# Seven weight slots per layer split by GpSimd, and nine matmuls of zeros ahead of the first real one

## The chip, the cores and the metric

The kernel runs on one core of a Trainium2 chip. The time is that of the device for one execution, in microseconds; before the change the median of three runs is 840.27 us (839.91 to 840.84).

The core has five engines with queues of their own: TensorE (PE in the rows; its weight loads are PEld), VectorE (DVE), ScalarE (ACT), GpSimd (POOL) and SyncE (SP), which here only issues DMAs. Each works through its instructions in order, and waits on semaphores for the others.

## What is computed

A trunk of two layers over 512 tokens of width 1024, all in float32. Cut to the part that matters here:

```python
for l in range(DEPTH):                                   # 2
    h = x @ w_in[l]
    c_q, c_kv, k_r, gate_a, q_d, k_d, v_d, gate_b, gates = _split_cols(h)
    q_a = (_rms_norm(c_q, g_q[l]) @ w_q_up[l]).reshape(b, s, MLA_HEADS, MLA_NOPE + MLA_ROPE)
    ...
    kv = (_rms_norm(c_kv, g_kv[l]) @ w_kv_up[l]).reshape(b, s, MLA_HEADS, MLA_NOPE + MLA_V)
    ...
    o_a = _dense_attention(...)                          # 8 heads, latent attention
    y_a = o_a * jax.nn.silu(gate_a) @ w_branch_a[l]
    ...
    o_b = _differential_attention(...)                   # 4 heads, two softmax maps each
    y_b = _rms_norm(o_b, g_diff[l], eps=1e-5) * (1.0 - lam_init) * jax.nn.silu(gate_b) @ w_branch_b[l]
    merged = g[..., :D_MODEL] * y_a + g[..., D_MODEL:] * y_b
    x = _layer_norm(DEEPNORM_ALPHA * x + merged @ w_out[l], ln_gamma[l], ln_beta[l])
```

## The kernel before

Every float32 factor is kept as an upper part, rounded to the format that TensorE multiplies (F32R), and a lower part, which is the factor less its upper part. A product is then three matmuls (`mm3`, L140): upper by upper, upper by lower, lower by upper. So each weight and each intermediate has to be split: ScalarE copies it to the upper part, and another engine subtracts.

**Weights.** All large weights are packed into slots of 128 x 1024, named in `SLOTS`: ga0 to ga3 are the gate of the latent attention, qd and kd the queries and keys of the differential attention, kvup and qup the up-projections, vd, gb, gt, br and o the rest. `slot` (L124) loads a slot into a raw buffer `wr` (two of these), copies it to `wh` on ScalarE (L127) and subtracts twice, 512 columns each, into `wl` on VectorE (L130); `wh` and `wl` have three buffers each. `proj` multiplies a slot by x: 8 chunks of three matmuls. A raw buffer is free for the next load when the copy and both subtractions are done.

**Beginning.** VectorE clears a tile, and TensorE multiplies it with itself seven times (L110 and L111), before there is any input. Then, chunk by chunk of x and of the latent weights, `load_x` and `load_wc` load and split, and `project` runs twelve matmuls of 128 x 416 a chunk: four tiles of 128 tokens, three matmuls each.

**Latent stage.** For each tile of tokens ScalarE sums the squares (L255, L256), VectorE adds the epsilon (L257, L258), GpSimd raises to the power -0.5 (L259), and ScalarE and VectorE scale (L261, L262). Transposes follow.

**Attention.** The steps of the string `STEPS` run in the order in which they are written: Q, K, s, t and v are queries, keys, scores, transposes and values of the latent attention's heads, q, k, w and b load and project for the differential one, S, T and V are its attention, and g, m, G and M are gates and merges. The steps a1, q0, k0, q1, k1, a2 and a3, which load the slots of the change, stand among the latent attention's. A score tile goes from TensorE to VectorE (maximum, L196), ScalarE (exponential, L198), TensorE (transpose, L205), ScalarE and VectorE (split, L207 and L208), and TensorE again (L371, L372).

**Layer boundary.** The output columns are multiplied, VectorE normalizes each tile of tokens, with a power on GpSimd (L633), stores it, and `feature_major` (L643) transposes it, split into x's parts (L652, L653). The last two tiles of layer 0 are transposed between the projections of layer 1's first tiles.

**The order on the engines.** The code gives dependencies and the order of the steps; a scheduler of the framework then decides the order in which instructions stand on each engine. So a change of one instruction's engine also moves its neighbours.

GpSimd has had, until now, only the powers (L259, L478, L633) and the DMAs of `bcast` (L163, L167), which write a row of sums to memory and read it back to all partitions.

Of the kernel before, what the change touches and what calls it, by code (L numbers as in the profile page):

```python
# [14 lines left out]
ALU = mybir.AluOpType  # L15
# [50 lines left out]
def hybrid_trunk(ctx: ExitStack, tc: tile.TileContext, x, xT, wlat, wts, prm, dlam, gb, tab, rtab, out):  # L66
    nc = tc.nc
# [9 lines left out]
    def nm(s):  # L77
        uid[0] += 1
        return f"{s}_{uid[0]}"
# [3 lines left out]
    def t2(tag, dt=F32, w=512):  # L83
        return sb.tile([P, w], dt, tag=tag, name=nm(tag), bufs=BUFS[tag])
# [6 lines left out]
    def pt_(tag):  # L91
        return ps.tile([P, 512], F32, tag=tag, name=nm("ps" + tag), bufs=PB[tag])

    def fr(ap):
        return ap.bitcast(F32)
# [11 lines left out]
    zero = t2("p", mybir.dt.bfloat16)  # L107
    nc.vector.memset(zero, 0.0)
    warm = pt_("sc")
    for i in range(7):  # L110
        nc.tensor.matmul(warm, lhsT=zero[:, 0:P], rhs=zero, start=True, stop=True)  # L111

    xH = cst.tile([P, KC, SEQ], F32R, name="xH")
# [5 lines left out]
    def load(src):  # L119
        raw = t2("wr", F32, 1024)  # L120
        nc.sync.dma_start(raw, src)
        return raw

    def slot(l, name):  # L124
        raw = load(wts[l, SLOTS.index(name)])
        hi, lo = t2("wh", F32R, 1024), t2("wl", F32R, 1024)
        nc.scalar.copy(hi, raw)  # L127
        for i in range(0, 1024, 512):
            c = slice(i, i + 512)
            nc.vector.tensor_tensor(lo[:, c], raw[:, c], fr(hi[:, c]), ALU.subtract)  # L130
        return hi, lo


# [11 lines left out]
    def proj(l, name, tag="acc"):  # L145

        hi, lo = slot(l, name)
        acc = pt_(tag)
        for k in range(KC):
            mm3(acc, hi[:, k * P:(k + 1) * P], lo[:, k * P:(k + 1) * P],  # L150
                xH[:, k, :], xL[:, k, :], k == 0, k == KC - 1)
        return acc
# [58 lines left out]
    def layer(l, last):  # L211
# [207 lines left out]
        def diff_v(c):  # L419

            ws = [slot(l, f"vd{c}{i}") for i in range(2)]
            out = []
            for hf in range(2):
                acc = pt_("acc")
                for i in range(2):
                    tk = slice((2 * hf + i) * P, (2 * hf + i + 1) * P)
                    for k in range(KC):
                        o = (k % 4) * 256
                        mm3(acc[:, i * 256:(i + 1) * 256], xH[:, k, tk], xL[:, k, tk],
                            ws[k // 4][0][:, o:o + 256], ws[k // 4][1][:, o:o + 256], k == 0, k == KC - 1)  # L430
                out.append(split(acc, "kv"))
            return out
# [58 lines left out]
        def branch(which, c, ys):  # L491
            if c % 2 == 0:
                br[which] = slot(l, f"br{'AB'[which]}{c // 2}")
            bhh, bll = br[which]
            acc = pt_("acc")
            for k in range(4):
                o = ((c % 2) * 4 + k) * P
                mm3(acc, bhh[:, o:o + P], bll[:, o:o + P], ys[k][0], ys[k][1], k == 0, k == 3)
            return acc
# [258 lines left out]
def _build(arrays):  # L758
    import concourse.bacc as _bacc
    nc = _bacc.Bacc("TRN2", target_bir_lowering=False, num_devices=1)  # L760
    args = [nc.dram_tensor(f"in_{n}_dram", arrays[n].shape, F32, kind="ExternalInput").ap() for n in _INS]
    args.append(nc.dram_tensor("out_0_dram", (SEQ, DM), F32, kind="ExternalOutput").ap())
    with tile.TileContext(nc) as tc:
        hybrid_trunk(tc, *args)
    return nc
# [9 lines left out]
```

## Time and profile before

| | |
|---|---|
| median of three runs | 840.27 us |
| the profiled execution, its own time | 840.24 us |
| its span, first to last instruction | 838.3 us |
| mean granted TensorE clock | 0.998 |
| VectorE, all 192 subtractions of `slot` | 127.3 us |
| ScalarE, all 96 copies of `slot` | 101.1 us |
| GpSimd, busy in all | 47.1 us |

A row of a group reads: line, engine, operation, output <- inputs, shapes, count | busy time, mean ns of one | idle time of the engine ahead of them, and who ended it. A row of a timeline begins with start and duration in us. A row of a stretch is its bounds, its length and the busy time (and number of instructions) of TensorE, its weight loads, VectorE, ScalarE and GpSimd, then the granted clock, the share of the DMA engines, and GB/s. L with a number is the line of the kernel before.

Busy time of TensorE is modelled to each matmul's end, and matmuls overlap: a 128 x 512 one takes 389 ns by its row, and the next starts some 230 ns behind it.

### The profile page before, as it was taken

Reading aid. Unit: us, or ns where it says so; the run is one execution under the profiler, and the core shown is the slowest. Engines: PE = TensorE matmul, PEld = TensorE weight load, DVE = VectorE, ACT = ScalarE, POOL = GpSimd, SP = SyncE. Lnnn points to the kernel's source line nnn. Section 1 sums busy time; section 2 is a strip of 40 time slices with the busy share of each in tenths; the row PEclk is TensorE's granted clock in tenths of the full one; section 3 lists DMA queues with packets and bytes.
Section 4 is the critical chain, followed back from the end, with each engine's and each line's share of the span. In section 5 each row is a group of like instructions: output and inputs, shape, how many; then the busy total and the mean of one; then the engine's idle time right before and its main releaser. Section 6 shows DMA issues by size and latency. Waiting matters only on the chain.

```text
span 838.3 us, 11089 instructions
## 1 busy us (share of the span) xinstructions
PE 828.4 (99%) x4095; PEld 693.1 (83%) x4095; DVE 590.0 (70%) x1070; ACT 430.0 (51%) x858; POOL 47.1 (6%) x70
## 2 busy tenths in 40 slices
PE   9999999999999999999999999999999999999996
PEld 7878888888898878888898787798888988788885
DVE  6789989667656664555867899887576566455657
ACT  5777777544624653333336787674454355433310
POOL 0100000000000011000110000000000001100001
PEclk9999999999999999999999999999999999999999
DMA  8411121222223263333532120122222323623222
GB/s 288 125 60 45 45 69 58 82 76 76 76 88 101 63 226 110 96 96 121 181 113 76 50 62 16 64 64 84 93 68 83 95 69 109 219 88 110 94 74 101
DMA packets 29622, 79.96 MB, mean 95 GB/s; under 512 B 4000, under 2 KB 8704, under 8 KB 29568
## 3 DMA queue, kind: packets, MB, share of 16 engines
q1 hardware_dynamic: 27648, 75.01, 28.4%
q0 software_dynamic: 1920, 4.25, 1.5%
q8 instruction: 32, 0.52, 0.2%
q14 instruction: 22, 0.18, 0.1%
HBM read 74.99 MB, written 4.24 MB: 95 GB/s over the span
## 4 chain that ended last, share of the span: by engine, by line
PE 96%; DMA 2%; DVE 1%; ACT 1%; issue 0%; DVEq 0%; SPq 0%; ACTq 0%; POOLq 0%
PE psacc L141 23%; PE psacc L142 23%; PE psacc L143 23%; PE pstr L205 5%; PE pssc L141 2%; PE pssc L142 2%; PE pssc L143 2%; PE pspv L371 2%; PE pspv L142 2%; PE pspv L372 2%; PE pspv L143 2%; PE pspv L141 2%; DMA tmp<-rows 1%; PE pssc L440 1%; PE pssc L444 1%; PE pssc L445 1%
## 5 line engine op out<-in xcount | busy, mean ns | idle before, releaser
L130 DVE TENSOR_TENSOR wl<-wr,wh 128x512 fp32r<-128x512 f32 x192 | 127.3, 686 | 101.0 <-ACT wh L127 94.4
L141 PE MATMUL psacc<-xH,wh 128*128 128x512 f32 x496 | 194.9, 393 | 0.0
L142 PE MATMUL psacc<-xL,wh 128*128 128x512 f32 x496 | 194.4, 392 | 0.0
L143 PE MATMUL psacc<-xH,wl 128*128 128x512 f32 x496 | 193.7, 390 | 0.0
L127 ACT CAST wh<-wr 128x1024 fp32r<-128x1024 f32 x96 | 101.1, 1053 | 144.3 <-PE psacc L142 106.9
L141 PEld LDWEIGHTS psacc<-xH,wh 128*128 128x128 f32 x496 | 93.2, 188 | 19.2
L143 PEld LDWEIGHTS psacc<-xH,wl 128*128 128x128 f32 x496 | 93.2, 188 | 19.0
L198 ACT ACTIVATE p<-pssc,sm 128x512 f32<-128x512 f32 x128 | 87.7, 688 | 41.1 <-DVE sm L196 40.6
L142 PEld LDWEIGHTS psacc<-xL,wh 128*128 128x128 f32 x496 | 93.2, 188 | 18.5
L196 DVE TENSOR_REDUCE sm<-pssc 128x1 f32<-128x512 f32 x128 | 85.0, 683 | 13.8 <-PE pssc L441 10.7
L208 DVE TENSOR_TENSOR pt<-pstr,pt 128x512 fp32r<-128x512 f32 x96 | 64.8, 684 | 3.1 <-ACT pt L207 2.5
L207 ACT CAST pt<-pstr 128x512 fp32r<-128x512 f32 x96 | 55.5, 585 | 18.0 <-PE pstr L205 15.0
L205 PE MATMUL pstr<-ident,p 128*128 128x128 f32 x384 | 57.6, 272 | 0.0
L205 PEld LDWEIGHTS pstr<-ident,p 128*128 128x128 f32 x384 | 47.1, 140 | 11.3 <-ACT p L198 1.1
L143 PE MATMUL psacc<-wh,xL 128*128 128x256 f32 x128 | 36.3, 284 | 0.0
L142 PE MATMUL psacc<-wl,xH 128*128 128x256 f32 x128 | 36.3, 284 | 0.0
L141 PE MATMUL psacc<-wh,xH 128*128 128x256 f32 x128 | 36.3, 284 | 0.0
L505 ACT ACTIVATE tmp<-psacc,bh 128x512 f32<-128x512 f32 x32 | 21.9, 684 | 11.7 <-DVE g L483 7.7
L371 PE MATMUL pspv<-pt,vs 128*128 128x512 f32 x64 | 27.1, 423 | 0.0
L163 POOL DMA_DIRECT2D rows<-tmp x16 | 9.1, 567 | 307.9 <-ACT tmp L161 307.9
L372 PE MATMUL pspv<-pt,vs 128*128 128x512 f32 x64 | 26.1, 407 | 0.0
L141 PE MATMUL pssc<-kv,qm 128*128 128x512 f32 x64 | 26.0, 421 | 0.0
(297 smaller groups left out, 1628.0 us busy)
## 6 DMA issues: line engine op xcount, KB each, us to landing
wr<-in_wts_dram SPq DMA_DIRECT2D x106, 512.0 KB, 3.5
p<-in_xT_dram SPq DMA_DIRECT2D x8, 256.0 KB, 5.3
qr<-in_wts_dram SPq DMA_DIRECT2D x16, 128.0 KB, 2.0
tmp<-rows POOLq DMA_DIRECT2D x16, 128.0 KB, 3.0
tmp<-rows POOLq DMA_DIRECT2D x8, 256.0 KB, 3.7
p<-in_gb_dram SPq DMA_DIRECT2D x8, 256.0 KB, 3.6
y<-in_x_dram SPq DMA_DIRECT2D x8, 256.0 KB, 5.8
x_scratch<-y SPq DMA_DIRECT2D x8, 256.0 KB, 2.1
```

The source lines that it names most:

```text
L127: nc.scalar.copy(hi, raw)
L130: nc.vector.tensor_tensor(lo[:, c], raw[:, c], fr(hi[:, c]), ALU.subtract)
L141: nc.tensor.matmul(o, lhsT=lh, rhs=rh, start=start, stop=False)
L142: nc.tensor.matmul(o, lhsT=lh, rhs=rl, start=False, stop=False)
L143: nc.tensor.matmul(o, lhsT=ll, rhs=rh, start=False, stop=stop)
L196: nc.vector.tensor_reduce(m, S, axis=AX.X, op=ALU.max, negate=True)
L198: nc.scalar.activation(p, S, AF.Exp, bias=m, scale=1.0, accum_out=sums)
L205: nc.tensor.transpose(b[:, t * P:(t + 1) * P], pts[t][:, c * P:(c + 1) * P], ident)
L207: nc.scalar.copy(h, b)
L208: nc.vector.tensor_tensor(lo, b, fr(h), ALU.subtract)
L371: nc.tensor.matmul(pv, lhsT=v, rhs=ph, start=kc == 0, stop=False)
L372: nc.tensor.matmul(pv, lhsT=v, rhs=pl, start=False, stop=kc == NT - 1)
```

## The change

```diff
-    for i in range(7):
+    for i in range(9):
         nc.tensor.matmul(warm, lhsT=zero[:, 0:P], rhs=zero, start=True, stop=True)
...
+    LATENT = ("ga1", "ga2", "ga3", "qd0", "qd1", "kd0", "kd1")
+
     def slot(l, name):
         raw = load(wts[l, SLOTS.index(name)])
+        eng = nc.gpsimd if name in LATENT else nc.vector
         hi, lo = t2("wh", F32R, 1024), t2("wl", F32R, 1024)
         nc.scalar.copy(hi, raw)
         for i in range(0, 1024, 512):
             c = slice(i, i + 512)
-            nc.vector.tensor_tensor(lo[:, c], raw[:, c], fr(hi[:, c]), ALU.subtract)
+            eng.tensor_tensor(lo[:, c], raw[:, c], fr(hi[:, c]), ALU.subtract)
```

The lower parts of seven slots in each layer, 14 subtractions of 128 x 512 a layer and 28 in all, are made by GpSimd, and TensorE begins with nine matmuls of zeros. The values stay the same. In the changed file all lines behind `load` stand four lower: L130 becomes L134, L259 becomes L263.

The scheduler moves other instructions with them. GpSimd's rows at the layer boundary before, where `sm` are the small tiles of statistics (L633 the normalization's powers of four tiles of tokens, L259 the latent stage's) and `rows` is the first broadcast of layer 1:

```order
L633 TENSOR_TENSOR sm_3902<-sm_3902,mhalf 128x1
L633 TENSOR_TENSOR sm_3940<-sm_3940,mhalf 128x1
L633 TENSOR_TENSOR sm_3978<-sm_3978,mhalf 128x1
L633 TENSOR_TENSOR sm_4030<-sm_4030,mhalf 128x1
L259 TENSOR_TENSOR sm_4147<-sm_4147,mhalf 128x2
L259 TENSOR_TENSOR sm_4195<-sm_4195,mhalf 128x2
L259 TENSOR_TENSOR sm_4229<-sm_4229,mhalf 128x2
L259 TENSOR_TENSOR sm_4263<-sm_4263,mhalf 128x2
L163 DMA rows_4685<-tmp_4683 8x128
```

The same place on GpSimd in the change, where wl_4356 is the lower part of ga1, wl_4622 of qd0, and the last three of kd0, qd1 and kd1:

```order
L637 TENSOR_TENSOR sm_3980<-sm_3980,mhalf 128x1
L134 TENSOR_TENSOR wl_4356<-wr_4353,wh_4355 128x512 x2
L637 TENSOR_TENSOR sm_4032<-sm_4032,mhalf 128x1
L134 TENSOR_TENSOR wl_4622<-wr_4619,wh_4621 128x512
L263 TENSOR_TENSOR sm_4149<-sm_4149,mhalf 128x2
L134 TENSOR_TENSOR wl_4622<-wr_4619,wh_4621 128x512
L263 TENSOR_TENSOR sm_4197<-sm_4197,mhalf 128x2
L263 TENSOR_TENSOR sm_4231<-sm_4231,mhalf 128x2
L263 TENSOR_TENSOR sm_4265<-sm_4265,mhalf 128x2
L134 TENSOR_TENSOR wl_4799<-wr_4796,wh_4798 128x512 x2
L134 TENSOR_TENSOR wl_5035<-wr_5032,wh_5034 128x512 x2
L134 TENSOR_TENSOR wl_5212<-wr_5209,wh_5211 128x512 x2
```

The last power of the normalization now stands behind ga1's two subtractions, and the first two powers of the latent stage stand behind one half each of qd0's.

ScalarE's rows at the same place before, where psacc_4053 and psacc_4054 are the latent projections of the first two tiles of tokens, pstr_4132 and pstr_4139 the transposes of x's third tile, pstr_4180 and pstr_4187 of its fourth and last:

```order
L255 ACTIVATE qm_4146,sm_4147<-psacc_4053 128x128
L652 CAST xH<-pstr_4132 128x4x128
L652 CAST xH<-pstr_4139 128x4x128
L256 ACTIVATE qm_4146,sm_4147<-psacc_4053 128x256
L261 ACTIVATE qm_4146<-psacc_4053,sm_4147 128x128
L127 CAST wh_4619<-wr_4617 128x1024
L652 CAST xH<-pstr_4180 128x4x128
L652 CAST xH<-pstr_4187 128x4x128
L255 ACTIVATE qm_4194,sm_4195<-psacc_4054 128x128
L256 ACTIVATE qm_4194,sm_4195<-psacc_4054 128x256
```

The same place on ScalarE in the change (all buffer numbers are two higher):

```order
L259 ACTIVATE qm_4148,sm_4149<-psacc_4055 128x128
L260 ACTIVATE qm_4148,sm_4149<-psacc_4055 128x256
L656 CAST xH<-pstr_4134 128x4x128
L656 CAST xH<-pstr_4141 128x4x128
L131 CAST wh_4621<-wr_4619 128x1024
L265 ACTIVATE qm_4148<-psacc_4055,sm_4149 128x128
L259 ACTIVATE qm_4196,sm_4197<-psacc_4056 128x128
L260 ACTIVATE qm_4196,sm_4197<-psacc_4056 128x256
L656 CAST xH<-pstr_4182 128x4x128
L656 CAST xH<-pstr_4189 128x4x128
```

The copy of qd0's upper part (L131) now stands ahead of the first scaling (L265), which waits for GpSimd, and the copies of x's last tile stand behind that scaling and behind the squares of the second tile.

## The prediction

> **What bounds the kernel now.** The page of the profile comes first: the span, the busy times and the chain that ended last.
>
> ```profile
> span 838.3 us, 11089 instructions
> PE 828.4 (99%) x4095; PEld 693.1 (83%) x4095; DVE 590.0 (70%) x1070; ACT 430.0 (51%) x858; POOL 47.1 (6%) x70
> PE 96%; DMA 2%; DVE 1%; ACT 1%; issue 0%; DVEq 0%; SPq 0%; ACTq 0%; POOLq 0%
> ```
>
> TensorE is busy for 828.4 of 838.3 us and makes up 96% of the chain. VectorE, which the change relieves, is at 70% and off the chain. So a microsecond taken from VectorE is worth nothing by itself; it counts only where TensorE waits for it, or for somebody who waits for it. The profiled execution took 840.24 us, 1.94 us more than its span, and stands 0.03 us under the median of the runs, 840.27. The sum below is made against 840.24.
>
> Busy time hides how fast TensorE runs, so the timeline of its first ten microseconds comes next (start, duration, instruction).
>
> ```profile
> 1.23 3.17 PE L111 MATMUL pssc<-p 128*128 128x512 bf16 x7 [1.23 <-DVE p L108]
> 5.14 0.71 PE L141 MATMUL psacc<-kv,xH 128*128 128x416 f32 x1 [0.75 <-ACT xH L137]
> 5.66 0.55 PE L142 MATMUL psacc<-kv,xH 128*128 128x416 f32 x1
> 6.00 0.55 PE L141 MATMUL psacc<-kv,xH 128*128 128x416 f32 x1
> ...
> 9.12 0.55 PE L143 MATMUL pspv<-kv,xL 128*128 128x416 f32 x1
> 9.47 0.41 PE L141 MATMUL psacc<-kv,xH 128*128 128x416 f32 x1
> 9.72 0.35 PE L142 MATMUL psacc<-kv,xH 128*128 128x416 f32 x1
> 9.91 0.35 PE L143 MATMUL psacc<-kv,xL 128*128 128x416 f32 x1
> ```
>
> Seven matmuls of zeros run from 1.23 to 4.40, then TensorE stands 0.75 us for the first chunk of x, then real work starts at 5.14. Up to 9.12 it starts a matmul every 0.35 us (5.66 to 6.00), from 9.72 on every 0.19 (9.72 to 9.91), the same shape. So the clock rises near 9.5, 4.33 us after unbroken work began at 5.14, and twelve real matmuls run slowly. (The granted clock reads 1.00 in this stretch already; the distances of the starts are what I go by.)
>
> The third view is the busy time by stretch for the two stages in which the moved subtractions mostly lie, and one later stage.
>
> ```profile
> 45.00:147.00 102.00, 102.00 (x530) 83.60 (x529) 94.14 (x167) 76.37 (x163) 6.53 (x12) 1.00 0.17 54
> 460.00:561.00 101.00, 101.00 (x526) 82.41 (x525) 92.54 (x165) 75.23 (x161) 6.40 (x12) 1.00 0.17 53
> 147.00:250.00 103.00, 103.00 (x536) 88.04 (x535) 67.59 (x125) 47.72 (x92) 2.21 (x3) 1.00 0.26 81
> ```
>
> The columns are the stretch, its length, then TensorE, weight loads, VectorE, ScalarE and GpSimd. VectorE is 92% busy in the latent attention of each layer, yet TensorE shows no idle time there.
>
> **Part 1, two more matmuls of zeros.** Seven take 3.17 us, so one every 0.43; nine end their starts at 1.23 + 9 x 0.43 = 5.1, where the first real one, which waits for ScalarE's copy of x, begins at 5.14 anyway. They cost 0.05 us at most and fill the pause of 0.75 us. If the clock needs unbroken work for 4.33 us, as it did after 5.14, it now rises at 1.23 + 4.33 = 5.56 and one or two real matmuls are slow instead of twelve. A slow one costs 0.35 - 0.19 = 0.16 us more. The bounds are nothing saved (the zeros or the pause play no part) and 12 x 0.16 = 1.9 us. One execution shows one delay only, and the three times of before differ by 0.93 us, as if the rise moved between runs; I take three slow ones left, nine saved: **-1.4 us**.
>
> The Trainium skill, "TensorE: Matmul & The Clock Gate", Part 1, says that the clock is released after one window of about 3.4 us of sustained work, and that the windows run freely, whenever the kernel starts. By that rule the rise would come anywhere from 3.4 to 6.8 us after unbroken work begins; the 4.33 us of the trace agrees, and the sum of this part would be about -1.3 us in the mean of runs, with a spread of more than a microsecond between them.
>
> Is the faster start fed? What the second and third chunk (twelve matmuls each) wait for last is in VectorE's timeline.
>
> ```profile
> 7.13 0.59 DVE L226 TENSOR_TENSOR kv<-y,kv 128x416 fp32r<-128x416 f32 x1 [0.35 <-ACT kv L225]
> 9.08 0.59 DVE L226 TENSOR_TENSOR kv<-y,kv 128x416 fp32r<-128x416 f32 x1
> 16.70 1.29 DVE L138 TENSOR_TENSOR xL<-p,xH 128x512 fp32r<-128x512 f32 x2
> ```
>
> They are there at 7.72 and 9.67; at full speed from about 6 the chunks begin near 7.8 and 10.1. The last two chunks of x are there at 17.99; the seventh begins at about 7.8 + 5 x 12 x 0.19 = 19.2. It is fed, and as TensorE sets the pace behind it, the gain stays.
>
> **Part 2, 28 subtractions move to GpSimd.** What VectorE loses, from the page's group and from the timeline around the last moved slot of layer 0, ga3:
>
> ```profile
> L130 DVE TENSOR_TENSOR wl<-wr,wh 128x512 fp32r<-128x512 f32 x192 | 127.3, 686 | 101.0 <-ACT wh L127 94.4
> 108.62 0.68 DVE L130 TENSOR_TENSOR wl<-wr,wh 128x512 fp32r<-128x512 f32 x1
> 109.22 0.69 DVE L187 TENSOR_TENSOR y<-op,y 128x512 fp32r<-128x512 f32 x1
> 111.73 0.64 DVE L130 TENSOR_TENSOR wl<-wr,wh 128x512 fp32r<-128x512 f32 x1
> 118.58 0.48 PE L141 MATMUL psacc<-xH,wh 128*128 128x512 f32 x1
> ```
>
> One takes 0.69 us and hands over after 0.60: 14 a layer free 8.4 us, of which seven, 4.2 us, lie in each stretch above (the others lie at 19 to 45 and 416 to 448). What that frees on TensorE is bounded by what it loses to late waits there. A matmul of this size that waits for nothing takes 389 ns, and the same groups with and without waits are:
>
> ```profile
> L371 PE MATMUL pspv<-pt,vs 128*128 128x512 f32 x64 | 27.1, 423 | 0.0
> L372 PE MATMUL pspv<-pt,vs 128*128 128x512 f32 x64 | 26.1, 407 | 0.0
> L141 PE MATMUL pssc<-kv,qm 128*128 128x512 f32 x64 | 26.0, 421 | 0.0
> L143 PE MATMUL psacc<-lat,wl 128*128 128x512 f32 x64 | 24.9, 389 | 0.0
> L440 PE MATMUL pssc<-qm,qm 128*128 128x512 f32 x32 | 13.5, 421 | 0.0
> L141 PE MATMUL pspv<-pt,kv 128*128 128x512 f32 x32 | 13.3, 417 | 0.0
> ACT p L198 <- DVE sm L196: 12.1, 16, 1.4
> ```
>
> The first three lose 64 x (34 + 18 + 32) ns = 5.4 us in both layers. ScalarE does wait for VectorE there (12.1 us in the first stretch, last row), so there is a way for the relief to reach TensorE. But the next two groups are the same kinds of matmul in the differential attention, most of it in stages like the third stretch, where VectorE is at 66%, and they lose as much (421) or nearly (417). So these losses hardly hang on VectorE's load. Between 0 and 5.4 us I take **-0.5 us**, near the end that the rows support.
>
> What GpSimd gains has no row in this profile: a 128x512 subtraction of two inputs. The nearest are VectorE's 0.69 us, and GpSimd's own:
>
> ```profile
> 1.02 0.29 POOL masks.py:199 TENSOR_SCALAR_AFFINE_SELECT ident<-ident 128x128 f32<-128x128 f32 x1
> 422.31 0.98 POOL L633 TENSOR_TENSOR sm<-sm,mhalf 128x1 f32<-128x1 f32 x1 [5.99 <-DVE sm L632]
> 426.88 1.18 POOL L259 TENSOR_TENSOR sm<-sm,mhalf 128x2 f32<-128x2 f32 x1 [3.59 <-DVE sm L258]
> ```
>
> From 0.29 us for 128 columns and one input come 1.16 for 512, twice that for two inputs, and with 0.98 as a fixed part 3.3 us. So one takes 0.69 to 3.3 us; I take 1.3, near the scaled row. The Trainium skill, "GPSIMD Engine Reference", 3.1, has 4.5 us for a 2048-wide addition; a quarter of it, an estimate from that page, is 1.1 us.
>
> A slot then takes 2.6 us instead of 1.3, and the cover is wide: ga3's halves end at 109.30 and 112.37 and are used from 118.58 on, and GpSimd, busy for 6.5 of 102 us, can start as soon as the upper part is cast. The narrow place is the layer boundary, where ga1's and half of qd0's subtraction now stand on GpSimd ahead of the RMS powers (order rows above):
>
> ```profile
> 417.35 1.05 ACT L127 CAST wh<-wr 128x1024 fp32r<-128x1024 f32 x1 [0.19 <-DVE y L639]
> 424.86 0.68 DVE L130 TENSOR_TENSOR wl<-wr,wh 128x512 fp32r<-128x512 f32 x1
> 428.10 0.37 ACT L261 ACTIVATE qm<-psacc,sm 128x128 f32<-128x128 f32 x1 [2.28 <-POOL sm L259]
> 429.43 1.05 ACT L127 CAST wh<-wr 128x1024 fp32r<-128x1024 f32 x1 [0.96 <-DMA wr<-in_wts_dram]
> 430.38 1.07 ACT L652 CAST xH<-pstr 128x512 fp32r<-128x512 f32 x2
> 434.21 0.35 PE L141 MATMUL pspv<-kv,xH 128*128 128x416 f32 x1
> ```
>
> Before, ga1's second half ends at 425.54, which frees its raw buffer; qd0's load follows and its cast runs at 429.43, 3.9 us after. Now, with p for one subtraction: ga1's cast ends at 418.40, GpSimd at 418.40 + 2p, the load has landed at 422.3 + 2p. On ScalarE the cast (1.05), then after GpSimd's half (p) and the power (1.18) the scaling (0.37), two squares (about 0.75) and the copy of x's last tile (1.07) follow, which TensorE needs at 434.21: 422.3 + 3p + 4.4 = 434.2 gives p = 2.5. At 1.3 there are over 2 us to spare, also behind the earlier casts; at 3.3 TensorE stands 3 x 0.8 = 2.4 us, once. At 1.3 this costs **0**. The loads of later slots are released earlier than before, which moves only SP's work.
>
> Sum: 840.24 - 1.4 - 0.5 = **838.3 us**.
>
> **The rivals.** A: the clock does not answer, because the zeros or the pause do not count; then only the relief is left, 840.24 - 0.5 = 839.8. Against it speaks that the rise follows the unbroken work by 4.33 us. B: the relief reaches TensorE well, with ScalarE's 12 us of waiting for VectorE as its way: two thirds of 5.4, 835.2. Against it speak 421 and 417. C, on the other side: while GpSimd subtracts, VectorE's operations with two inputs stand for the whole of it. VectorE then loses p and gains 0.60 seven times a stretch, and has 102 - 94.14 = 7.86 us of idle time: this decides from p = 0.60 + 7.86 / 7 = 1.7 us on. At 2.0 it falls behind by 1.9 us a stretch, 3.9 in both, and TensorE with it: 840.24 - 1.4 + 3.8 = 842.6. For it speaks the 92%; against it that much of VectorE's time there is work on one input, a quarter of it in the reductions alone:
>
> ```profile
> L196 DVE TENSOR_REDUCE sm<-pssc 128x1 f32<-128x512 f32 x36 | 24.2, 683 | 1.4 <-PE pssc L143 1.1 <-PE pssc L445 0.2
> ```
>
> The Trainium skill, "SBUF — State Buffer", "Who interferes with whom", states this as a rule: a VectorE instruction with two SBUF inputs and a GpSimd one that reads SBUF exclude each other for the whole instruction; no run here shows it yet. D: the new order of TensorE's rows and some of C's stops eat gain and relief, 840.0.
>
> **How the numbers follow.** Forecast 56%, A 17%, B 9%, C 8%, D 10%. A measurement tells 0.2%, 1.7 us, from no change: faster is below 838.6, slower above 841.9. The forecast's own range, 837.2 to 839.5, lies two thirds below 838.6, 37%; with B's 9 and 2 of A faster gets 48%. Slower is C, 8%; the rest, 44%, is the same. The range leaves out B and C, 17%: from 836.0, about halfway to B, to 841.2, which is the layer boundary's stop of 2.4 us at p = 3.3 with the relief lost (840.24 - 1.4 + 2.4).
>
> **What would show it.** Part 1: TensorE's starts 0.19 us apart from 5 to 7 us on, instead of 9.7, with no pause ahead of 5.14; the latent projection ends 1.4 us earlier. Part 2: 28 rows on POOL of 1.1 to 1.5 us each, L371 and L141 within a few ns of 423 and 421, and x's last tile copied ahead of its matmul at the layer boundary. Subtractions over 1.7 us, or VectorE's two-input rows longer than 0.69 us beside GpSimd's, would speak for C; slow starts still at 9 us for A.

## The result, and the profile after

| | before | the change |
|---|---|---|
| median, same chip | 840.13 us | 851.33 us (850.63 to 851.88, 4 runs) |
| ratio | | 1.0135, 95% interval 1.0123 to 1.0147 |
| profiled execution, own time | 840.24 us | 850.63 us |
| its span | 838.3 us | 848.8 us |

The change makes the kernel 11.2 us slower. Forecast were 838.3 us, 836.0 to 841.2. One execution of all those behind the tables of this document is left out, of 4389.4 us, in the run with qd0 of layer 0 and ga2 back.

The page of the change, span, busy times and chain:

```profile
span 848.8 us, 11108 instructions
PE 833.4 (98%) x4097; PEld 691.5 (81%) x4097; DVE 580.4 (68%) x1042; ACT 429.2 (51%) x858; POOL 84.0 (10%) x98
PE 87%; DVE 4%; DMA 2%; ACT 1%; issue 1%; DVEq 0%; SPq 0%; POOLq 0%; POOL 0%; ACTq 0%
L134 POOL TENSOR_TENSOR wl<-wr,wh 128x512 fp32r<-128x512 f32 x28 | 38.0, 1374 | 105.1 <-ACT wh L131 85.7
```

VectorE has 9.6 us less to do, and yet it now holds 4% of the chain instead of 1%: TensorE waits for an engine that is less busy than before. One subtraction on GpSimd takes 1.37 us in the mean, as guessed (1.3). The list of TensorE's waits in the change names the places (us in total, times, longest; the wait ahead of the zeros, 1.2 us as before, isn't shown):

```profile
PE pstr L296 <- DVE tmp L293: 2.4, 1, 2.4
PE pstr L209 <- DVE pt L212: 2.2, 2, 1.1
PE psacc L145 <- DVE tmp L349: 0.7, 1, 0.7
PE pspv L146 <- DVE pt L212: 0.6, 2, 0.5
```

Of these, the same list of before has only the fourth (0.8 us there). The longest stands at 29 us, in the beginning of layer 0. Its rows in the change's timeline (start, duration), and the two-input group of the same line before:

```profile
28.95 2.56 POOL L134 TENSOR_TENSOR wl<-wr,wh 128x512 fp32r<-128x512 f32 x2 [1.42 <-ACT wh L131]
29.16 2.51 DVE L293 TENSOR_TENSOR tmp<-tmp,tmp 128x128 f32<-128x128 f32 x2
31.72 0.63 PE L296 MATMUL pstr<-ident,tmp 128*64 128x128 f32 x4 [2.38 <-DVE tmp L293]
...
32.73 0.63 PE L147 MATMUL psacc<-xH,wl 128*128 128x512 f32 x1
33.15 0.63 PE L145 MATMUL psacc<-xH,wh 128*128 128x512 f32 x1
33.58 0.63 PE L146 MATMUL psacc<-xL,wh 128*128 128x512 f32 x1
```

```profile
30.80 0.48 DVE L289 TENSOR_TENSOR tmp<-tmp,tmp 128x128 f32<-128x128 f32 x2
```

Two additions of 128 columns, both inputs in SBUF, take 2.51 us beside the subtractions of qd0, and 0.48 without; the group ends at 31.67, 0.16 us behind GpSimd's pair (31.51). TensorE stands 2.38 us for them, and behind that its matmuls start 0.43 us apart (33.15 to 33.58) where 0.23 is usual: the clock has fallen to half.

The second place is ga2, in both layers alike. Rows of the change at 82 us, and of before where the same rotation (four lines lower in its numbers) stands:

```profile
81.67 2.98 POOL L134 TENSOR_TENSOR wl<-wr,wh 128x512 fp32r<-128x512 f32 x2 [8.31 <-ACT wh L131]
81.95 1.55 DVE L395 TENSOR_TENSOR tmp<-tmp,tabs 128x512 f32<-128x512 f32 x1
83.43 0.68 DVE L349 TENSOR_TENSOR tmp<-psacc,tabs 128x512 f32<-128x512 f32 x1
84.03 1.18 DVE L398 TENSOR_TENSOR tmp<-tmp,tmp 128x512 f32<-128x512 f32 x1
84.37 0.39 PE L146 MATMUL psacc<-lat,kv 128*128 128x512 f32 x1
85.86 0.66 PE L209 MATMUL pstr<-ident,p 128*128 128x128 f32 x4 [1.11 <-DVE pt L212]
```

```profile
77.90 0.68 DVE L391 TENSOR_TENSOR tmp<-tmp,tabs 128x512 f32<-128x512 f32 x1
79.10 0.68 DVE L394 TENSOR_TENSOR tmp<-tmp,tmp 128x512 f32<-128x512 f32 x1
```

The operation with two inputs in SBUF (L395) takes 1.55 instead of 0.68 us and so does not end before GpSimd's first subtraction has; L349, with one input in PSUM, runs at its usual 0.68 in the middle of GpSimd's second; L398, two inputs in SBUF again, waits for the second's end. GpSimd's pair is lengthened too, 2.98 instead of 2.56. The two lengthenings, 0.87 and 0.50 us, bring VectorE 1.4 us late to the next lower part (L212), and TensorE's starts lie 85.86 - 84.37 = 1.49 us apart instead of 0.23.

A third chain shows at 36 to 47 us, layer 0 alone, in the change's timeline over four engines:

```profile
36.20 2.55 POOL L134 TENSOR_TENSOR wl<-wr,wh 128x512 fp32r<-128x512 f32 x2 [4.68 <-ACT wh L131]
38.77 7.64 SPq L121 DMA_DIRECT2D wr<-in_wts_dram  x3
42.32 1.05 ACT L131 CAST wh<-wr 128x1024 fp32r<-128x1024 f32 x1 [1.37 <-DMA wr<-in_wts_dram]
43.28 0.57 ACT L324 CAST vs<-psacc 128x512 fp32r<-128x512 f32 x1
46.29 0.68 DVE L349 TENSOR_TENSOR tmp<-psacc,tabs 128x512 f32<-128x512 f32 x1
47.11 0.47 PE L145 MATMUL psacc<-lat,qw 128*128 128x512 f32 x1 [0.68 <-DVE tmp L349]
```

GpSimd ends kd0's pair at 38.75 and only then frees the raw buffer; SyncE issues the next load at 38.77, ScalarE waits 1.37 us for it in order to cast qd1, and the four copies of the values (L324), which the change's order puts behind that cast (in the second trace of before, three of the four stand ahead of it), wait with it, then VectorE's part of them, then TensorE. That this stop is GpSimd's doing alone isn't shown: in the runs below in which GpSimd only fills, and the raw buffer is free as soon as ScalarE has cast it, TensorE waits 0.6 to 0.7 us for the same product.

### The profile page after: what moved, and what is told of

It reads as the page before. It is cut to its first block, busy times and chain, and to the rows that moved or that the text cites. A ratio compares the mean times of both kernels' runs of the same rounds, so it can differ in the third digit from the quotient of the medians.

```text
span 848.8 us, 11108 instructions
## 1 busy us (share of the span) xinstructions
PE 833.4 (98%) x4097; PEld 691.5 (81%) x4097; DVE 580.4 (68%) x1042; ACT 429.2 (51%) x858; POOL 84.0 (10%) x98
## 4 chain that ended last, share of the span: by engine, by line
PE 87%; DVE 4%; DMA 2%; ACT 1%; issue 1%; DVEq 0%; SPq 0%; POOLq 0%; POOL 0%; ACTq 0%
PE psacc L147 22%; PE psacc L146 21%; PE psacc L145 21%; PE pstr L209 4%; PE pssc L145 2%; PE pspv L375 2%; PE pssc L146 2%; PE pssc L147 2%; PE pspv L376 2%; PE pspv L146 2%; PE pspv L147 1%; PE pspv L145 1%; DMA tmp<-rows 1%; PE pssc L448 1%; PE pssc L444 1%; PE pssc L445 1%
## 5 line engine op out<-in xcount | busy, mean ns | idle before, releaser
L131 ACT CAST wh<-wr 128x1024 fp32r<-128x1024 f32 x96 | 101.0, 1053 | 154.7 <-PE psacc L146 115.7
L134 DVE TENSOR_TENSOR wl<-wr,wh 128x512 fp32r<-128x512 f32 x164 | 108.3, 686 | 99.5 <-ACT wh L131 93.5
L212 DVE TENSOR_TENSOR pt<-pstr,pt 128x512 fp32r<-128x512 f32 x96 | 64.6, 683 | 4.5 <-ACT pt L211 3.8
L134 POOL TENSOR_TENSOR wl<-wr,wh 128x512 fp32r<-128x512 f32 x28 | 38.0, 1374 | 105.1 <-ACT wh L131 85.7
L482 POOL TENSOR_TENSOR sm<-sm,mhalf 128x4 f32<-128x4 f32 x8 | 9.8, 1228 | 228.5 <-DVE sm L480 228.4
L375 PE MATMUL pspv<-pt,vs 128*128 128x512 f32 x64 | 27.0, 422 | 0.5 <-ACT pt L211 0.2
```

The costliest lines, as they stand in the source:

```text
L134: eng.tensor_tensor(lo[:, c], raw[:, c], fr(hi[:, c]), ALU.subtract)
L212: nc.vector.tensor_tensor(lo, b, fr(h), ALU.subtract)
L375: nc.tensor.matmul(pv, lhsT=v, rhs=ph, start=kc == 0, stop=False)
```

## The experiments

Two theories stood against each other. The **hold**: while GpSimd reads SBUF in a subtraction, VectorE's operations with two inputs in SBUF stand until it ends (with the later release of raw buffers as its companion). The **order**: the scheduler, given other durations, places matmuls of TensorE ahead of what feeds them.

All runs, each beside the kernel before on the same chip:

| run | time | before | ratio, 95% interval |
|---|---|---|---|
| before, again | 838.97 | 838.68 | |
| nine zeros alone | 839.42 | 839.00 | 1.0005 (0.9996 to 1.0015) |
| GpSimd alone, seven zeros | 851.61 | 839.00 | 1.0146 (1.0131 to 1.0161) |
| qd0 of layer 0 back | 847.27 | 839.00 | 1.0096 (1.0081 to 1.0111) |
| qd0 of layer 0 and ga2 back | 844.01 | 839.42 | 1.0056 (1.0039 to 1.0073) |
| GpSimd copies one input | 844.67 | 839.00 | 1.0065 (1.0048 to 1.0081) |
| pieces of 128 columns | 853.33 | 838.68 | 1.0177 (1.0162 to 1.0192) |
| transposes in the pause | 851.41 | 839.42 | 1.0145 (1.0128 to 1.0162) |
| old order, GpSimd subtracts | 849.14 | 838.68 | 1.0122 (1.0107 to 1.0137) |
| old order, GpSimd fills | 846.10 | 839.42 | 1.0080 (1.0059 to 1.0102) |
| the same, GpSimd's order too | 840.91 | 839.57 | 1.0021 (1.0011 to 1.0030) |
| new order, GpSimd fills | 843.96 | 839.42 | 1.0056 (1.0041 to 1.0071) |
| new order, VectorE subtracts | 849.27 | 838.68 | 1.0123 (1.0106 to 1.0140) |

### The zeros alone, and before once more

```diff
-    for i in range(7):
+    for i in range(9):
```

> The kernel before with nine matmuls of zeros and nothing else. My reading of the changed kernel's first ten microseconds is that this part works: the clock rises at 5.25 instead of 9.59 us, and the starts of the first 10 us lose 1.84 instead of 4.28 us. So 840.2 - 2.4 = 837.8 us, between 837.4 and 838.9. If the early clock is worth nothing because later stages wait for something else, 840.2. If the loss of the change came from the zeros, near 851.

> The kernel before, unchanged, for a second trace. If the rise of the clock hangs on the pause ahead of the first real matmul, it comes near 9.6 us again and the first 10 us lose about 4.4 us. If it moves between executions, as the same seven zeros with a rise at 6.53 us in the run without the two further ones suggest, it may come anywhere from 4.7 to 9.6 us, and then the two zeros bring nothing that can be measured, as their run alone shows (839.42 against 839.0 us).

Nothing: the two zeros alone move the time by +0.4 us, not told from none. The second trace of before suggests why. Its timeline of TensorE:

```profile
1.22 3.17 PE L112 MATMUL pssc<-p 128*128 128x512 bf16 x7 [1.22 <-DVE p L109]
4.71 0.71 PE L142 MATMUL psacc<-kv,xH 128*128 128x416 f32 x1 [0.32 <-ACT xH L138]
5.57 0.54 PE L142 MATMUL psacc<-kv,xH 128*128 128x416 f32 x1
5.92 0.39 PE L143 MATMUL psacc<-kv,xH 128*128 128x416 f32 x1
6.52 0.35 PE L142 MATMUL psacc<-kv,xH 128*128 128x416 f32 x1
6.70 0.35 PE L143 MATMUL psacc<-kv,xH 128*128 128x416 f32 x1
...
30.19 0.52 PE L293 MATMUL pstr<-ident,tmp 128*64 128x128 f32 x3 [0.47 <-DVE tmp L290]
```

With the same seven zeros the starts are 0.35 us apart at 5.57 and 0.18 at 6.52: the clock rises near 6, and not at 9.5 as in the execution on which the prediction stood. The pause ahead of the first real matmul is 0.32 us here and was 0.75 there. And where TensorE comes early to 29 us, it waits 0.47 us for the rotated keys; with nine zeros, whose list of waits follows, 0.6:

```profile
PE pstr L292 <- DVE tmp L289: 0.6, 1, 0.6
```

### GpSimd alone

```diff
-    for i in range(9):
+    for i in range(7):
```

> The change without its two further zeros: only the subtractions on GpSimd. If the two parts add up, 851.3 + 2.4 = 853.7 us. If the stop of 2.4 us at 29 us depends on TensorE arriving there 2 us earlier than before, it shrinks to about 0.5 us, the clock does not fall behind it, and the time is 853.7 - 1.9 - 1.6 = 850.2 us or less. If GpSimd's subtractions cost nothing, 840.

851.61 us, +12.6: the loss is that of the moved subtractions. The clock rose early here as well, near 6.5 us, so TensorE didn't come to 29 us two microseconds later, and the second case of the expectation wasn't tried: it waits 2.3 us there. The busy time by stretch (the granted clock is the third number from the end):

```profile
25.00:36.00 11.00, 8.68 (x48) 7.10 (x47) 8.22 (x20) 7.35 (x20) 4.43 (x5) 1.00 0.22 69
45.00:52.00 7.00, 5.48 (x17) 4.08 (x17) 6.61 (x13) 3.63 (x9) 1.22 (x1) 0.76 0.36 115
```

After nearly the same pause as in the change (2.32 us instead of 2.38) the clock stays up here, and falls one stop later; the last section says where the two pauses differ.

### Slots taken back

```diff
-        eng = nc.gpsimd if name in LATENT else nc.vector
+        eng = nc.gpsimd if name in LATENT and (l, name) != (0, "qd0") else nc.vector
```

> The changed kernel with one slot, qd0 of layer 0, back on VectorE. By the theory that VectorE's operation with two inputs stands for the whole of GpSimd's pair, the stop of 2.4 us at 29 us and the half clock behind it (1.6 us) are gone, and perhaps the two later waits of 0.8 and 0.6 us that layer 1 doesn't have: 851.3 - 4.0 = 847.3 down to 845.9 us; the two-input group at 29 us takes 0.5 instead of 2.51 us. If the new order of the engines costs the time, one slot of 14 brings about 1 us at most: 850.3 to 851.3.

Two subtractions of 28 taken back bring the loss from 11.2 to 8.3 us, near the theory's 847.3; the clock stays up. The two-input group at 29 us takes 0.49 us, as expected; TensorE still waits 1.0 us for it, as VectorE's own subtraction of qd0 now stands ahead of it. With ga2 back as well:

```diff
+        eng = nc.gpsimd if name in LATENT and name != "ga2" and (l, name) != (0, "qd0") else nc.vector
```

> The changed kernel with qd0 of layer 0 and ga2 of both layers back on VectorE, the three pairs at 29, 82 and 499 us. If these holds make most of the loss, 847.3 (qd0 alone) less the two waits of 1.1 us and the blips behind them (1.3 each): 844.7 us. If other holds take their place, or the loss lies in the order, 846 to 848 us.

844.0 us, against 844.7 expected: 4.6 us are left, while 22 subtractions are still on GpSimd. So three pairs make more than half of the loss. What remains isn't in the holds at 29 and 82 us. (The scheduler places other instructions anew in both runs, so they don't part the hold from the order by themselves.)

### What holds VectorE

```diff
+            if name in LATENT:
+                nc.gpsimd.tensor_copy(lo[:, c], fr(hi[:, c]))
```

> The changed kernel with GpSimd copying the upper part where it subtracted, so with one input instead of two; the lower parts of these slots are wrong. If what holds VectorE is that both engines read two inputs, no operation of VectorE's is longer beside GpSimd, the stops at 29, 84 and 501 us go, and the time is 851.3 - 2.4 - 1.6 - 2.6 = 844.7 us or less. If any reading of GpSimd's holds VectorE, the rows at 29 and 82 us are as long as GpSimd's pair of copies, whatever that takes. If the order of the engines costs the time, 851 as before, with no long rows.

The time is that of the first case, but the rows are those of the second. Rows of GpSimd and VectorE in this run:

```profile
30.75 1.27 POOL L135 CAST wl<-wh 128x512 fp32r<-128x512 f32 x2 [1.40 <-ACT wh L131]
30.97 1.19 DVE L296 TENSOR_TENSOR tmp<-tmp,tmp 128x128 f32<-128x128 f32 x2
```

A copy with one input holds VectorE's two-input operations as well, 1.19 instead of 0.48 us; it just takes half as long as the subtraction. The idea that both engines must read two inputs falls: on GpSimd's side one is enough. With zeros filled in, where GpSimd only writes, the same group runs at its own pace beside it (the last of the runs below, in the old order with GpSimd's order too):

```profile
29.56 0.99 POOL L184 MEMSET wl<- 128x512 f32 x2 [0.25 <-PE pssc L199]
29.99 0.49 DVE L345 TENSOR_TENSOR tmp<-tmp,tmp 128x128 f32<-128x128 f32 x2
```

This is the rule of the Trainium skill, "SBUF — State Buffer", "Who interferes with whom", that the prediction named: a VectorE instruction with two SBUF inputs and a GpSimd instruction that reads SBUF, not one that only writes it, exclude each other. These rows agree in both halves.

Cutting the subtractions up:

```diff
+        n = 128 if name in LATENT else 512
+        for i in range(0, 1024, n):
```

> The changed kernel with GpSimd's subtractions cut into pieces of 128 columns, eight instead of two a slot. If an operation of VectorE with two inputs waits for the end of one GpSimd instruction, it now waits for a quarter of the time: the wait at 29 us falls from 2.4 to about 1 us, the clock stays up (1.6), the waits at 84 and 501 us fall from 1.2 to about 0.4 us: 851.3 - 1.4 - 1.6 - 1.6 = 846.7 us. If VectorE gets through only when GpSimd has no more work, the waits stay and the time is 851 us or, since more instructions take longer, above.

Rows of VectorE, TensorE and ScalarE in this run:

```profile
29.27 0.90 DVE L294 TENSOR_TENSOR tmp<-tmp,tmp 128x128 f32<-128x128 f32 x2
30.23 0.63 PE L297 MATMUL pstr<-ident,tmp 128*64 128x128 f32 x4
44.86 1.04 ACT L131 CAST wh<-wr 128x1024 fp32r<-128x1024 f32 x1 [4.69 <-DMA wr<-in_wts_dram]
```

The mechanism is as expected: the hold lasts for one instruction of GpSimd's, so the group takes 0.90 us and the stop at 29 us is gone. The time is not: eight pieces take 3.4 to 3.9 us where two take 2.56, the raw buffer comes free later, and ScalarE's cast of qd1 now waits 4.7 us for its load, with the copies of the values behind it. TensorE stands 4.0 us there and the clock falls with it (0.66 over 45 to 55 us). The third chain, 0.7 us of waiting in the change, is the dearest here.

### The half clock

```diff
+        for _ in range(20 if l == 0 else 0):
+            nc.tensor.transpose(b[:, 0:P], ident, ident)
```

> The changed kernel, in its own order, with 20 transposes of the identity ahead of the rotated keys' (L300), where TensorE stands 2.4 us for VectorE; they write where the real ones write afterwards. They take 2.2 us, so TensorE works where it stood, and goes on no sooner. If the half clock from 32.6 to 36.0 us follows from the pause, it is gone and the time falls by 1.6 us: 849.7 us on a chip where the change takes 851.3, and 0.5 to 1.6 less in the mean if not every execution loses the clock. If the clock falls for another reason, nothing changes, or it rises by a few tenths.

No gain. The busy time by stretch in the change:

```profile
25.00:36.00 11.00, 8.62 (x39) 6.84 (x38) 8.08 (x20) 7.13 (x19) 4.04 (x5) 0.84 0.24 73
45.00:52.00 7.00, 6.32 (x28) 4.57 (x26) 6.61 (x15) 3.46 (x9) 1.06 (x1) 1.00 0.38 115
```

and with the transposes:

```profile
25.00:36.00 11.00, 11.00 (x68) 9.59 (x67) 8.03 (x20) 7.15 (x18) 4.00 (x5) 1.00 0.20 73
45.00:52.00 7.00, 5.48 (x18) 4.07 (x17) 6.38 (x13) 2.86 (x6) 1.05 (x1) 0.76 0.36 115
```

In the change the clock is 0.84 over 11 us, 11 x 0.16 = 1.8 us lost. With TensorE busy in the pause it stays at 1.00. But that the transposes did this isn't shown: in the run of GpSimd alone the clock stayed at 1.00 as well, with the pause of 2.32 us left as it was. What both runs show is the next stop. At 45 to 47 us TensorE waits 1.52 us for the same product of VectorE's instead of 0.68, because that chain runs over GpSimd, SyncE and ScalarE and not over TensorE, and behind this wait the clock falls there (0.76 over 7 us, 1.7 us). Two stops in a row, each on a chain of its own: what is saved at the first is lost again at the second.

### Order and hold apart

The change gives 855 of TensorE's 4097 matmuls another place than the nine zeros alone do. To part this from the hold, edges between neighbours keep TensorE, ScalarE and VectorE in a given order, whichever engine subtracts; `ORDER` is a table of instruction names, of the nine zeros alone (old) or of the change (new).

```diff
+def keep_order(tc):
+    by = {i.name: i for i in tc.nc.cur_bb.bb.instructions}
...
+            if prev is not None:
+                tc.add_manual_dep(ins, prev.name, info, reason="order")
+            prev = ins
...
         hybrid_trunk(tc, *args)
+        keep_order(tc)
```

> The change with the order of the kernel before: edges hold TensorE, ScalarE and VectorE to the very order that they have when VectorE subtracts all slots and nine zeros stand ahead, while GpSimd makes the 28 subtractions. What is left is GpSimd's hold on VectorE. By the theory of the hold: the wait at 29 us is 2.4 instead of 0.6 us (+1.8), the half clock behind it +1.6 where it falls, the waits at 82 and 499 us +1.2 each, so 839.4 + 5.8 = 845.2 us (843 to 847). If the new order made the loss: 839.4 us. If both do: what this run lacks to 851 is the order's.

> The other half: all subtractions on VectorE and nine zeros, but TensorE, ScalarE and VectorE are held to the order that the change gave them (only the 28 subtractions find their own place on VectorE). No GpSimd subtraction, so no hold. By the theory of the hold the order costs little: 839.4 plus the small losses of 0.2 to 0.3 us that the change shows in both layers alike, 1.5 and 2.0 us in the run with copies: 840.5 to 843 us. If the order is the cause, it is near 850 us. Since VectorE has its subtractions back, it may come later than in the change's own order would have it, which would add to this.

Both lose as much as the change: +10.5 and +10.6 us. The first shows that the new order isn't needed for the loss. It also lies above the 843 to 847 expected: in the old order the holds strike at more places, kd1's among them in both layers, here on GpSimd and VectorE:

```profile
65.48 3.04 POOL L182 TENSOR_TENSOR wl<-wr,wh 128x512 fp32r<-128x512 f32 x2 [18.62 <-ACT wh L179]
67.29 1.78 DVE L443 TENSOR_TENSOR tmp<-tmp,tabs 128x512 f32<-128x512 f32 x1
```

The second, expected at 840.5 to 843, misses: an order made for a relieved VectorE suffers when VectorE has the work back (in the same order, with VectorE relieved and GpSimd only filling, 4.5 us are lost below and not 10.6), so that run doesn't give the order's share. For that, GpSimd fills with zeros and reads nothing, in either order:

```diff
+            if name in LATENT:
+                nc.gpsimd.memset(fr(lo[:, c]), 0.0)
```

> As the run with the order of the kernel before (849.1 us), but GpSimd fills the 28 half slots with zeros where it subtracted, so it reads nothing; the lower parts of these slots are left out. VectorE has no more work than there. If the loss comes from what GpSimd's reading does (VectorE's two-input operations stand, the raw buffers come free later), all of it goes: 839.4 us, or down to 838 if VectorE's relief is worth something. If it comes from GpSimd's being late or from the change in VectorE's load, it stays near 849.

> The same with the order that the change gave to TensorE, ScalarE and VectorE: VectorE is relieved, as that order assumes, and nothing holds it. If the order itself costs nothing, 839.4 us as in the run before this; if its small losses of 0.2 to 0.3 us are its own, 840.5 to 842; if the order makes the change's loss, about 850.

In the new order +4.5 us remain, between the second and the third case; GpSimd's own rows aren't held in that run, but TensorE waits nowhere in it for more than 0.7 us behind the beginning. The run in the old order, 846.1 us instead of 839.4, had two stops for which GpSimd's fill of ga3, which stood ahead of a broadcast's DMAs, was to blame by the trace. So once more, with GpSimd's rows in the order in which it subtracted:

> The run with zeros filled in and the order of the kernel before, once more, but GpSimd too is held to the order of the run in which it subtracted (849.1 us). In the first such run (846.1 us) a fill stood ahead of a broadcast's DMAs on GpSimd and made two stops of 2.6 and 3.0 us, at 98 and 515 us, with the half clock behind each; everywhere else its starts lost no more than with all subtractions on VectorE. If those stops were a matter of GpSimd's order alone, the time is now 838.5 to 840 us: then all of the loss in the old order comes from GpSimd's reading. If it stays near 846, something else in the moved work costs it.

840.91 us, a little above the 838.5 to 840 expected: what is left of those stops is 0.9 us at 100 us and a smaller one in layer 1. Then:

| loss against before, us | GpSimd reads (subtracts) | GpSimd only writes (fills) |
|---|---|---|
| old order | 10.5 | 1.3 |
| new order | 11.2 | 4.5 |

Each number is good to about a microsecond, and a difference of two to one and a half. With fills none of VectorE's operations is longer beside GpSimd than by itself. So without its reading, GpSimd's work costs 1.3 us in the old order; the reading, with the raw buffers that it keeps and the longer time that it takes (2.56 us a pair instead of 0.99), costs 9.1 there and 6.7 in the new. That the lower parts come later isn't it: in none of these runs' lists of waits does TensorE wait for one of GpSimd's. The new order costs 3.2 us by itself, and gives most of it back when GpSimd reads, as it avoids kd1's holds. None of these kernels is faster than the one before.

## Why the prediction was wrong, point by point

**Part 1, the zeros (-1.4 us).** Wrong in size: +0.4, not told from none. Two steps failed. "If the clock needs unbroken work for 4.33 us, as it did after 5.14" took one execution's late rise for the rule; the bound of nothing saved was there, but 9.5 us was the exception: in the two other traces with seven zeros the clock rises near 6 and near 6.5. The rise in the change itself came as forecast, as TensorE's rows there show:

```profile
4.89 0.61 PE L145 MATMUL psacc<-kv,xH 128*128 128x416 f32 x1
5.34 0.35 PE L146 MATMUL psacc<-kv,xH 128*128 128x416 f32 x1
5.53 0.35 PE L145 MATMUL psacc<-kv,xH 128*128 128x416 f32 x1
```

so that its profile, beside the one of before, looks as if the part had paid. And "as TensorE sets the pace behind it, the gain stays" fails at 29 us: the chain of scalings and rotations on ScalarE, GpSimd and VectorE was just behind TensorE, and takes back 0.5 to 0.6 us of the lead in the second trace of before and in the run of the zeros alone. The check of the feed ended with x's last chunk, one stage too early.

**Part 2, VectorE's relief (-0.5 us).** No gain was measured: with the old order, VectorE without the 28 subtractions and GpSimd reading nothing, the time is 1.3 us above before. The argument that those matmuls hardly depend on VectorE's load agrees with the change: the groups of 423 and 421 ns read 422 and 431 in the change:

```profile
L375 PE MATMUL pspv<-pt,vs 128*128 128x512 f32 x64 | 27.0, 422 | 0.5 <-ACT pt L211 0.2
L145 PE MATMUL pssc<-kv,qm 128*128 128x512 f32 x64 | 26.3, 431 | 0.6 <-ACT p L202 0.4
```

**Part 2, GpSimd's time (1.3 us).** Right: 1.37.

**Part 2, the cover.** At the layer boundary, called the narrow place, it holds: TensorE has no wait there in the change. "The cover is wide" was read from ga3's use of `wl` alone, and is wrong in layer 0, where the raw buffer goes round from GpSimd over SyncE to ScalarE with nothing to spare (42.32). It is the loop worked out for the boundary, applied at one place instead of at each. (With fills TensorE waits 0.6 to 0.7 us there as well, so the loop has little to spare even without GpSimd in it.)

**Rival C (842.6 us, 8%)** had the mechanism, which the sum put at nothing, and is the step that failed most: "this decides from p = 0.60 + 7.86 / 7 = 1.7 us on" asks whether VectorE has idle time enough over a hundred microseconds. VectorE never ran out of time; its load fell. What counts is whether the one operation that is held is the next thing that TensorE waits for. At p = 1.3 that was so three times, for 2.4, 1.1 and 1.1 us of waiting, and the first one cost the clock for another 1.8: 6.4 us together, where the reading costs 6.7 in the same order by the table above. The rest of the 11.2 us is the 3.2 of the order and the 1.3 that stay with fills. The rival's own sum is also a little off: the second stretch has 101 - 92.54 = 8.46 us of idle time, so at p = 2.0 VectorE would fall behind by 1.9 and 1.3 us, 3.3 in all and not 3.8. (And 838.6 lies 61% up the forecast's own range, so its part below is 34% and not 37%.) The objection that much of VectorE's work has one input is right (L349 passes freely) and doesn't help, since a rotation holds two operations with two.

**Rival D, the new order (840.0)** was undersized: with VectorE relieved and nothing held the time is 4.5 us above before, of which 3.2 are the order's.

**The clock.** The prediction dealt with it at the start only. In the change a pause of 2.4 us in mid-kernel halves it for 3.4 us. The Trainium skill, "TensorE: Matmul & The Clock Gate", Part 1, has it fall after an idle window of about 3.4 us; here less than that of idleness was enough, and the measurement decides.

What stays open: which of the moved rows make the 3.2 us of the new order wasn't taken apart, nor how the 9.1 us in the old one divide between held operations and late raw buffers. That the pauses of this kernel make the clock fall rests on where the falls lie in the traces (last section); no run kept everything else and filled a pause behind which the clock would have fallen.

## What to carry to other kernels

Before an elementwise operation goes to GpSimd, look at what VectorE runs at that moment: if an operation with two inputs in SBUF stands there and TensorE waits for its result soon, up to the whole of GpSimd's instruction is added to the path, as at 29 us, however idle VectorE is over the stage. Follow a buffer's release over every queue at each place where the buffer goes round, not only at the narrowest one. And take a second trace of before, ahead of counting on an event that a single execution shows.

## What the runs showed of the hardware that was not expected

Beside VectorE's two-input operations, a copy with one input on GpSimd is as exclusive as a subtraction (1.19 us instead of 0.48), and a fill isn't at all (0.49). The two engines pass the right by single instructions, so each of VectorE's operations waited for one of GpSimd's, and GpSimd's pair grew in turn from 2.56 to 2.98 us.

A pause of TensorE of 2.38 us made the clock fall in the change, one of 2.32 us did not in the run of GpSimd alone, and there the next stop, shorter than that, did. The traces show in what they differ. In every trace the changes of the clock lie whole multiples of 3.413 us apart: in the change it rises at 5.25 us, falls 8 of them later, at 32.55, and rises one later, at 35.97. Two rows by stretch (bounds, length, TensorE's busy time first, the clock third from the end) from that trace:

```profile
29.14:32.55 3.41, 1.03 (x8) 0.78 (x7) 3.39 (x4) 1.14 (x3) 2.38 (x2) 1.00 0.23 46
32.55:35.97 3.42, 3.42 (x13) 2.64 (x12) 1.48 (x3) 2.34 (x4) 0.00 (x0) 0.50 0.53 184
```

Counted in such steps from the first rise on, the full clock fell in the traces of this case behind each step in which TensorE stood for 1.78 us or more, and behind none in which it stood for 1.69 or less. The change's pause lies within one step. That of GpSimd alone is cut in two by the end of a step, 0.63 and 1.69 us, and its next stops, 0.26 and 1.52 us, fall into one, 1.78 together. So which of two like pauses is hit depends on where they lie in the steps, and not on their length alone; and where the steps lie differs from one execution to the next, as the first rise does.
